# Two transformer blocks on one core: modulation scaled on ScalarE, attention divided at the end, gate work one expert pair earlier

## The chip, the core and the metric

The kernel runs on one NeuronCore of a Trainium2 chip. Five engines work side by side, each with its own queue that is served in order: TensorE (PE; its weight loads are PEld), VectorE (DVE), ScalarE (ACT), GpSimd (POOL), and SyncE (SP), which here only issues transfers. The metric is the device time of one execution in microseconds, the median of the runs. All matrices are fp32. Where a product of two matrices has to be exact, each factor is split into a rounded part and a rest (types `fp32r`), and three fast products take the place of one slow one.

## The reference

512 tokens of width 1024 go through two blocks. Cut to what matters here:

```python
mod = silu(c) @ ada_w + ada_b                  # six vectors of 1024: shifts, scales, gates
h = rmsnorm(x, g) * (1 + sc_a) + sh_a
# four mixers of four heads each: diff, forgetting ("fox"), stick-breaking, sparse ("nsa")
# forgetting attention, for a block of 128 queries:
s = q @ k.T * scale + (cum[query] - cum[key])  # cum: running sum of log forget gates
p = softmax(where(key <= query, s, NEG));  o = p @ v
x = x + gt_a * (concat(o_a, o_b, o_c, o_d) @ w_out)
x = x + gt_m * conv_ffn(rmsnorm(x) * (1 + sc_m) + sh_m)
# second block: pooling mixer and neighbourhood attention (softmax(s + bias) @ v), then
x = x + expert_choice_ffn(...)                 # 16 experts, 64 tokens each, silu(xe@wg) * (xe@wu) @ wd
g = sigmoid(rms_norm(x) @ w_ple_gate);  e = rms_norm(p @ w_ple_proj)
x = x + g * e                                  # gated embedding
```

## The kernel before

**Modulation.** The first 2048 columns of `ada_w` are done at the start. The other 4096 come as 64 tiles of 128 x 512 (`ada_more`, L349): SP loads tile `adw` (two buffers), POOL multiplies it by a column of `cT` (L355), and copies it into the accumulator `ada_a` (L358, first of each eight; one buffer) or adds it (L360). After eight tiles four small matmuls `pm` (L364) sum over the partitions. 48 tiles are spread over the mixers by `ada_side`, 16 belong to the loop of the conv FFN.

**Mixers of block one.** Eight cores (a mixer with two of its four heads) run two at a time as generators; between their steps, projections (`ftile`) of later mixers are recorded. A softmax goes: scores on PE; DVE adds the bias and finds the row minimum (`softmax_part`, L616); ACT takes the exponential and its row sum (L618); DVE forms 1/sum (L639) and scales the probabilities (`scale_parts`, L643); PE transposes them (`pt`), DVE or ACT copies them out of PSUM, PE multiplies by the values (`od`). In `fox` (L851) DVE also builds each bias in a tile `fb`: the key's running sum minus the query's (L861), and the causal mask on the last 128 keys (L862).

**Norms of heads.** `rstd_rows` (L379) makes one reciprocal root per token and group; with four groups it calls the six small instructions of `rstd_of` (L372 to L377) twice, for eight columns each. `to_features` (L388) lays such numbers along the free axis: a DVE copy to 128 x 512 (L393), four PE transposes into `rb` (L397).

**Block two.** Neighbourhood attention (`na`, L1184) has the same softmax chain, with 248 or 256 keys in a block.

**Experts.** Sixteen experts run as eight pairs, numbered 0 to 7; the two of a pair use the two column halves of PE side by side. A pair takes 48 weight chunks of 1 MB from HBM, loaded by SP into rings of buffers (`chy`, `chr`, `x16`, `chl`), 64 + 32 couples of matmuls (`ga`, `ua`, then `yd`), a scatter of its result to the tokens (`po`, `spread`), and the gather of the next pair's tokens `xg` (POOL, `route`). Beside that, in steps that `between` takes after each two chunks, goes the work of the gated embedding, in the list `todo`: `embedding()` in pair `E_AT`; `gate_base(t)` in the pairs of the table `BASE`, 16 couples of matmuls `pg` (L1553) of the tokens' state with the gate's weights `w_pg`; and `gate_pair`, from the first pair in `BASE` on, 16 couples `z` of the pair's own result with the same weights, scattered to those tokens whose base was taken before. `PACE` says how many steps `between` takes in each pair. From pair `RETIRE` on the six `chr` buffers hold `w_pg` and the gate's sums in place of chunks; POOL scales `w_pg` once (L1565). From pair `HOLD` = 4 on, these steps are tied behind the pair's own matmul in the recorded order; in earlier pairs the scheduling layer may move them.

**What sets the order.** Instructions are recorded in program order with priorities (`high_priority` shifts them), and a scheduling layer fixes each engine's queue from that before the run. Waits between engines are by semaphores; an engine stops at the first instruction whose input or buffer is not there.

Of the kernel before, what the change touches and what calls it, by code (L numbers as in the profile page):

```python
# [230 lines left out]
def _build(ctx, tc, nc, a, dbg, stop):  # L231
# [147 lines left out]
    def rstd_rows(sq, ind, n, scale, tag="dense"):  # L379
# [5 lines left out]
        for c in range(0, 4 * n, 8):  # L385
            rstd_of(ms[:, c:min(c + 8, 4 * n)], scale, y[:, c:min(c + 8, 4 * n)])
# [464 lines left out]
    def fox(hp):  # L851
        q, kk, v, ckb = st["fox", hp]
        o = ps("od", "o", 2)
        for i in range(4):
# [945 lines left out]
```

## Time and profile before

| | us |
|---|---|
| three runs | 2103.95, 2106.22, 2110.03; median 2106.22 |
| profiled execution, its own time | 2106.01 |
| its span, first to last instruction | 2104.2 |
| busy in the span: PE, DVE, ACT, POOL | 1904.4, 851.3, 555.5, 243.8 |
| start (norm, first projections) | 0 to 60 |
| mixers of block one and the second half of their output product | 60 to 470 |
| conv FFN | 470 to 850 |
| mixers of block two | 850 to 985 |
| output product, router | 985 to 1070 |
| expert pairs 0 to 7 | 1070 to 2074 |
| last gate and output | 2074 to 2104 |

Busy time is time in which an engine worked on an instruction; matmuls are pipelined, so a busy PE is not PE at its peak. The stages were told apart by the tiles in the timeline. In the rows below, `L643 DVE TENSOR_SCALAR e<-e,r` is an instruction of line 643 on DVE that writes tile `e` from `e` and `r`; `x64` says how many; behind the first bar stand their busy time and the mean of one in ns, behind the second the engine's idle time just before them and what ended most of it. The clock is the share of TensorE's full clock that was granted in the stretch.

### The profile page before, as it was taken

What the parts mean: (1) busy time and instruction counts of PE and PEld (TensorE: products, weight loads), DVE (VectorE), ACT (ScalarE), POOL (GpSimd) and SP (SyncE); (2) the same over time, 40 slices, a digit from 0 to 9 for tenths busy, and PEclk for the clock granted to TensorE, in tenths of its full rate; (3) what the DMA queues carried; (4) which work ended last, traced back from release to release, by engine and by line L of the source; (5) the groups of instructions that cost most, each with busy time, mean ns of one, the idle gap of its engine ahead of it and who ended that gap; (6) DMA issues with size and microseconds to landing.
All of it is one profiled execution on the core that took longest, in us unless ns stands there. A gap on an engine that the chain in (4) does not pass through costs nothing.

```text
span 2104.2 us, 22827 instructions
## 1 busy us (share of the span) xinstructions
PE 1904.4 (91%) x8822; PEld 1067.6 (51%) x8822; DVE 851.3 (40%) x1761; ACT 555.5 (26%) x1089; POOL 243.8 (12%) x211
## 2 busy tenths in 40 slices
PE   2898988979999999999989988988779999999997
PEld 1566656658888887777643322322223333333343
DVE  7887887875444335677441101210010020110114
ACT  4655544534323324445310000200000000100012
POOL 5540333350200000000100000000030000000001
PEclk9998998989999999999989999999989999999998
DMA  6532223333322223222589999899999999999991
GB/s 245 167 116 66 86 81 93 108 101 105 112 107 92 100 91 100 76 79 77 237 357 421 422 422 420 368 420 419 421 419 395 420 385 367 418 390 396 401 387 68
DMA packets 95084, 523.67 MB, mean 249 GB/s; under 512 B 11405, under 2 KB 12853, under 8 KB 44032
## 3 DMA queue, kind: packets, MB, share of 16 engines
q1 hardware_dynamic: 89936, 501.53, 60.9%
q0 software_dynamic: 3552, 17.82, 2.3%
q10 hardware_dynamic: 1488, 2.87, 0.4%
q8 instruction: 69, 1.13, 0.2%
q14 instruction: 39, 0.32, 0.0%
HBM read 510.83 MB, written 4.27 MB: 245 GB/s over the span
## 4 chain that ended last, share of the span: by engine, by line
PE 67%; DMA 18%; DVE 10%; ACT 2%; issue 2%; POOL 0%; SPq 0%; DVEq 0%; POOLq 0%; ACTq 0%
DMA ch<-in_w_ue_dram 8%; DMA ch<-in_w_de_dram 6%; PE ua L1697 5%; PE ga L1697 4%; PE ga L1698 4%; PE yd L1728 4%; PE yd L1727 3%; PE pg L1553 3%; PE z L1553 2%; PE ag L332 2%; PE ag L333 2%; PE ag L334 2%; PE od L649 2%; PE av L332 2%; PE av L333 2%; PE av L334 2%
## 5 line engine op out<-in xcount | busy, mean ns | idle before, releaser
L1697 PE MATMUL ga<-ch,xe 128*64 128x512 f32 x512 | 242.5, 610 | 9.0 <-DMA ch<-in_w_ge_dram 9.0
L1698 PE MATMUL ua<-ch,xe 128*64 128x512 f32 x512 | 231.1, 596 | 21.4 <-DMA ch<-in_w_ue_dram 21.4
L1728 PE MATMUL yd<-ch,hts 128*64 128x512 f32 (+1 forms) x544 | 233.5, 576 | 16.4 <-DMA ch<-in_w_de_dram 16.3
L1698 PE MATMUL ga<-ch,xe 128*64 128x512 f32 x512 | 236.5, 607 | 5.4 <-DMA ch<-in_w_ge_dram 5.4
L1727 PE MATMUL yd<-ch,hts 128*64 128x512 f32 (+1 forms) x544 | 234.8, 576 | 0.0
L1697 PE MATMUL ua<-ch,xe 128*64 128x512 f32 x512 | 233.5, 596 | 0.0
L325 DVE TENSOR_TENSOR wlo<-pan,whi 128x1024 fp32r<-128x1024 f32 x119 | 156.1, 1312 | 159.2 <-ACT whi L322 154.0
L322 ACT ACTIVATE whi<-pan 128x1024 fp32r<-128x1024 f32 x119 | 125.9, 1058 | 212.9 <-PE ag L333 93.8
L1708 DVE TENSOR_TENSOR sg<-sg,ua 128x512 f32<-128x512 f32 x32 | 22.0, 686 | 265.4 <-PE ua L1698 265.4
L1728 PEld LDWEIGHTS yd<-ch,hts 128*64 128x64 f32 x544 | 72.2, 138 | 110.4 <-issue 75.4
L1698 PEld LDWEIGHTS ga<-ch,xe 128*64 128x64 f32 x512 | 67.2, 139 | 93.3 <-issue 78.5
L1698 PEld LDWEIGHTS ua<-ch,xe 128*64 128x64 f32 x512 | 67.4, 137 | 88.7 <-issue 52.3
L1697 PEld LDWEIGHTS ua<-ch,xe 128*64 128x64 f32 x512 | 67.0, 137 | 77.0 <-issue 74.6
L338 DVE TENSOR_TENSOR ys<-yg,ys 128x512 fp32r<-128x512 f32 (+1 forms) x17 | 12.5, 733 | 229.9 <-ACT ys L337 229.9
L1697 PEld LDWEIGHTS ga<-ch,xe 128*64 128x64 f32 x512 | 66.0, 139 | 66.1 <-issue 54.0
L1727 PEld LDWEIGHTS yd<-ch,hts 128*64 128x64 f32 x544 | 71.6, 138 | 50.3 <-issue 47.9
L1687 ACT ACTIVATE hts<-pth 128x512 f32<-128x512 f32 x32 | 19.1, 596 | 266.9 <-PE pth L1686 266.9
L1731 ACT ACTIVATE yg<-yd,gs 128x512 f32<-128x512 f32 (+1 forms) x17 | 11.3, 662 | 287.2 <-PE yd L1728 196.3
L355 POOL TENSOR_TENSOR adw<-adw,cT 128x512 f32<-128x512 f32 x64 | 77.7, 1215 | 40.5 <-DMA adw<-in_ada_dram 40.3
L360 POOL TENSOR_TENSOR ada_a<-ada_a,adw 128x512 f32<-128x512 f32 x56 | 78.3, 1399 | 4.4
L1707 ACT ACTIVATE sg<-ga 128x512 f32<-128x512 f32 x32 | 19.1, 597 | 224.0 <-PE ga L1698 224.0
L618 ACT ACTIVATE e<-e,m 128x256 f32<-128x256 f32 (+8 forms) x128 | 65.1, 509 | 49.4 <-DVE m L616 46.9
(896 smaller groups left out, 3833.8 us busy)
## 6 DMA issues: line engine op xcount, KB each, us to landing
ch<-in_w_de_dram SPq DMA_DIRECT2D x128, 1024.0 KB, 13.7
ch<-in_w_ue_dram SPq DMA_DIRECT2D x125, 1024.0 KB, 9.9
ch<-in_w_ge_dram SPq DMA_DIRECT2D x120, 1024.0 KB, 13.4
pan<-in_w_up_dram SPq DMA_DIRECT2D x44, 512.0 KB, 3.2
adw<-in_ada_dram SPq DMA_DIRECT2D x64, 256.0 KB, 2.6
pan<-in_w_in_dram SPq DMA_DIRECT2D x24, 512.0 KB, 3.7
pan<-in_w_dn_dram SPq DMA_DIRECT2D x22, 512.0 KB, 3.2
adr<-in_adaT_dram SPq DMA_DIRECT2D x8, 1024.0 KB, 9.2
```

Source lines behind the costliest of these rows:

```text
L322: A.activation(hi, raw, AF.Copy)
L325: eng.tensor_tensor(lo, raw, hi.bitcast(FT), op=OP.subtract)
L332: T.matmul(out, wh, xh, start=first, stop=False)
L333: T.matmul(out, wh, xl, start=False, stop=False)
L334: T.matmul(out, wl, xh, start=False, stop=last)
L355: P.tensor_tensor(w, w, cT[:, k:k + 1].to_broadcast([128, 512]), op=OP.mult)
L360: P.tensor_tensor(ada_next[1], ada_next[1], w, op=OP.add)
L1553: T.matmul(out[c_], w[:, c_], x_, start=start, stop=stop)
L1697: T.matmul(acc_[m][0:64], xe[:, kk, 0:64], wa[:, k], start=kk == 0, stop=kk == 7)
L1698: mm = T.matmul(acc_[m][64:128], xe[:, kk, 64:128], wb[:, k], start=kk == 0, stop=kk == 7)
L1727: T.matmul(yd[0:64], hts[:, kk, 0:64], wa[:, k_], start=kk == 0, stop=kk == 15)
L1728: mm = T.matmul(yd[64:128], hts[:, kk, 64:128], wb[:, k_], start=kk == 0, stop=kk == 15)
```

## The change

Modulation: ACT multiplies the tile by the column (as the scale of a copy), writing the first of each eight straight into the accumulator; POOL keeps the additions. Forgetting attention: the query's term, the same for all keys of a row, is left out of the bias, since a softmax does not change with it; the mask is added once for both heads, into the key's tile, which makes the order of query blocks 3, 2, 1, 0. Forgetting and neighbourhood attention: the probabilities are not scaled; `divided` multiplies the output of all blocks by the reciprocals at the end, laid along the free axis by `to_features`. Norms: sixteen columns at a time. Experts: the tables move the gate's weights, bases and gating from pairs 4 to 7 to pairs 3 to 6 (gating still runs to pair 7), and the embedding from pair 2 to pair 1.

```diff
-RETIRE = 4
-BASE = {4: [0], 5: [1], 6: [2], 7: [3]}
-E_AT = 2
+RETIRE = 3
+BASE = {3: [0], 4: [1], 5: [2], 6: [3]}
+E_AT = 1
-PACE = [1.0, 1.0, 1.0, 1.0, 2.2, 2.2, 2.2, 2.2]
+PACE = [1.0, 1.0, 1.0, 2.2, 2.2, 2.2, 2.2, 1.5]
...
-            P.tensor_tensor(w, w, cT[:, k:k + 1].to_broadcast([128, 512]), op=OP.mult)
             if k == 0:
                 ada_next[1] = tmp[0].tile([128, 512], FT, name="ada_a", tag="ada_a", bufs=1)
-                P.tensor_copy(ada_next[1], w)
+                A.activation(ada_next[1], w, AF.Copy, scale=cT[:, 0:1])
             else:
+                A.activation(w, w, AF.Copy, scale=cT[:, k:k + 1])
                 P.tensor_tensor(ada_next[1], ada_next[1], w, op=OP.add)
...
-        for c in range(0, 4 * n, 8):
-            rstd_of(ms[:, c:min(c + 8, 4 * n)], scale, y[:, c:min(c + 8, 4 * n)])
+        rstd_of(ms[:, 0:4 * n], scale, y)
...
+    def divided(o, l, out):
+
+        A.activation(out, o, AF.Copy)
+        r = sm([128, 8], "r8", 2)
+        V.reciprocal(r, l)
+        V.tensor_tensor(out, out, to_features(r, 2), op=OP.mult)
...
     def fox(hp):
-        for i in range(4):
+        ls_ = sm([128, 4, 2], "l8", 2)
+        for i in (3, 2, 1, 0):
             nk = 128 * (i + 1)
+            V.tensor_tensor(ckb[:, :, nk - 128:nk], ckb[:, :, nk - 128:nk], K["cm"].unsqueeze(1).to_broadcast([128, 2, 128]),
+                            op=OP.add)
             for par in range(2):
-                h = 2 * hp + par
-                fb = t2k("fb")
-                V.tensor_scalar(fb[:, :nk], ckb[:, par, :nk], cqc[:, 4 * i + h:4 * i + h + 1], None, op0=OP.subtract)
-                V.tensor_tensor(fb[:, nk - 128:nk], fb[:, nk - 128:nk], K["cm"], op=OP.add)
                 s = ps("s", "s", 2)
                 scores(s, q, kk, par, slice(128 * i, 128 * i + 128), 0, nk)
-                e.append(softmax_part(s, fb[:, :nk], nk, l[:, par:par + 1]))
+                e.append(softmax_part(s, ckb[:, par, :nk], nk, ls_[:, i, par:par + 1]))
             yield
-            scale_parts(e, l, nk)
...
-        A.activation(mix[:, 2 + hp], o, AF.Copy)
+        divided(o, ls_.rearrange("p i h -> p (i h)"), mix[:, 2 + hp])
...
     def na(hp):
-            scale_parts(e, l, nk)
...
+        t = p2k("on")
+        divided(o, l.rearrange("p i h -> p (i h)"), t)
```

How the queues move, at the three places that the prediction speaks of. VectorE in forgetting attention of block one, before (`fb` is the bias, `e,m<-s,fb` the minimum, `r` and `e` of L641 and L643 belong to the sparse mixer beside it):

```order
L641 TENSOR_TENSOR r_3359<-r_3359,gates 128x2
L643 TENSOR_SCALAR e<-e,r_3359 128x31 x2
L634 COPY pts<-pt 31x128
L861 TENSOR_SCALAR fb<-ckb,cqc 128x128
L862 TENSOR_TENSOR fb<-fb,cst 128x128
L616 ISA e,m<-s,fb 128x128
L616 ISA m 128x1
```

and now (`ckb` is the key's tile with the mask):

```order
L615 ISA e,m<-s,ckb 128x256
L615 ISA m 128x1
L638 RECIPROCAL r_3019<-l_2921 128x2
L863 TENSOR_TENSOR ckb<-ckb,cst 128x2x128
L640 TENSOR_TENSOR r_3019<-r_3019,gates 128x2
L642 TENSOR_SCALAR e<-e,r_3019 128x384 x2
```

The two bias instructions ahead of each minimum became one mask addition per block; the scaling that is left is that of the sparse mixer. ScalarE at the end of the mixers, where the output product's panels are split (`whi`) and the squares for the next norm are taken (`sq`), before:

```order
L923 ACTIVATE mix<-od 128x512
L337 ACTIVATE hTh<-mix 128x512
L322 ACTIVATE whi<-pan 128x1024
L408 ACTIVATE sq<-x 128x512 x3
L322 ACTIVATE whi<-pan 128x1024
L408 ACTIVATE sq<-x 128x512 x2
```

and now:

```order
L337 ACTIVATE hTh<-mix 128x512
L322 ACTIVATE whi<-pan 128x1024
L357 ACTIVATE ada_a<-adw,cT 128x512
L359 ACTIVATE adw<-adw,cT 128x512 x2
L407 ACTIVATE sq<-x 128x512
L322 ACTIVATE whi<-pan 128x1024
L359 ACTIVATE adw<-adw,cT 128x512
L407 ACTIVATE sq<-x 128x512
```

Eight modulation tiles, recorded for the loop of the conv FFN, stand between the squares and panels. TensorE where pair 3 begins, before (`po` scatters the pair before):

```order
L1728 MATMUL yd<-ch,hts 64x512
L1697 MATMUL ga<-ch,xe 64x512
L1537 MATMUL po<-ys,ott 128x512 x4
L1698 MATMUL ga<-ch,xe 64x512
L1697 MATMUL ga<-ch,xe 64x512
```

and now (`ptg` turns the tokens of a base, `pg` is the base's product):

```order
L1731 MATMUL yd<-ch,hts 64x512
L1540 MATMUL po<-ys,ott 128x512 x8
L1606 MATMUL ptg<-cst,xk 128x128 x8
L1556 MATMUL pg<-ch 64x512 x17
L1700 MATMUL ga<-ch,xe 64x512
L1556 MATMUL pg<-ch 64x512 x6
L1701 MATMUL ga<-ch,xe 64x512
```

More than half of the first base's 32 matmuls stand ahead of the pair's first own matmul. On GpSimd the eight scalings of `w_pg`, one run of eight before, now stand in runs of two, two and four, with the gather of pair 4's tokens and the copies that wait for it in between.

## Rows read from the trace of the kernel before

**Rows 1.** Stretches: us, busy us of PE, PEld, DVE, ACT, POOL; clock, DMA share, GB/s.
```profile
60.00:470.00 410.00, 356.63 (x1884) 256.81 (x1884) 328.44 (x814) 205.89 (x496) 147.75 (x118) 0.94 0.31 99
850.00:985.00 135.00, 133.54 (x692) 102.89 (x692) 97.89 (x253) 63.15 (x144) 1.61 (x3) 1.00 0.25 80
```

**Rows 2.** Chain of waits, 60 to 470: share of the stretch by engine and line.
```profile
by line: PE od L649 6.1%; PE pt L627 5.6%; issue 3.7%; DVE e L643 3.6%; PE ms L383 3.2%; DVE wlo L325 3.1%; PE s L817 2.4%; DVE e L616 2.4%; PE od L920 2.3%; DVE e L706 1.8%; DVE q L576 1.6%; PE rb L397 1.4%; DVE fb L862 1.3%; DVE sq L410 1
```

**Rows 3.** Groups by line, VectorE, 60 to 470: busy us, mean ns, idle before.
```profile
L325 DVE TENSOR_TENSOR wlo<-pan,whi 128x1024 fp32r<-128x1024 f32 x31 | 44.8, 1444 | 5.7 <-issue 2.7 <-ACT whi L322 2.6 <-PE acc__1241 L334 0.3
L643 DVE TENSOR_SCALAR e<-e,r 128x128 f32<-128x128 f32 (+7 forms) x64 | 32.9, 550 | 0.6
L410 DVE TENSOR_TENSOR sq<-sq 128x512 f32<-128x512 f32 x7 | 10.4, 1479 | 2.2 <-ACT sq L408 2.2
L861 DVE TENSOR_SCALAR fb<-ckb,cqc 128x128 f32<-128x128 f32 (+3 forms) x16 | 9.0, 560 | 0.0
L862 DVE TENSOR_TENSOR fb<-fb,cst 128x128 f32<-128x128 f32 x16 | 8.4, 526 | 0.3
L376 DVE TENSOR_TENSOR rv<-rv,ry 128x8 f32<-128x8 f32 (+2 forms) x19 | 3.7, 201 | 0.3
L568 DVE SCALAR_TENSOR_TENSOR sq<-pr,cols,rb 128x512 f32<-128x512 f32 x5 | 3.7, 741 | 0.9 <-PE rb L397 0.9
```

**Rows 4.** The same view, VectorE, 850 to 985.
```profile
L325 DVE TENSOR_TENSOR wlo<-pan,whi 128x1024 fp32r<-128x1024 f32 x16 | 19.5, 1220 | 0.4 <-ACT whi L322 0.2
L643 DVE TENSOR_SCALAR e<-e,r 128x248 f32<-128x248 f32 (+1 forms) x22 | 6.8, 345 | 0.1
L393 DVE COPY bc<-rs 128x512 f32<-128x512 f32 x8 | 3.4, 426 | 0.2
L568 DVE SCALAR_TENSOR_TENSOR sq<-pr,cols,rb 128x512 f32<-128x512 f32 x4 | 3.0, 740 | 0.6 <-PE rb L397 0.6
```

**Rows 5.** The same view, VectorE, 818 to 850.
```profile
L410 DVE TENSOR_TENSOR sq<-sq 128x512 f32<-128x512 f32 x7 | 4.9, 694 | 0.0
```

**Rows 6.** The same view, GpSimd, 60 to 470.
```profile
L355 POOL TENSOR_TENSOR adw<-adw,cT 128x512 f32<-128x512 f32 x58 | 69.4, 1198 | 38.3 <-DMA adw<-in_ada_dram 38.2
L360 POOL TENSOR_TENSOR ada_a<-ada_a,adw 128x512 f32<-128x512 f32 x49 | 69.3, 1414 | 3.8
L358 POOL COPY ada_a<-adw 128x512 f32<-128x512 f32 x7 | 6.7, 958 | 182.9 <-PE pm L364 182.9
```

**Rows 7.** The same view, ScalarE, 60 to 470.
```profile
L408 ACT ACTIVATE sq<-x 128x512 f32<-128x512 f32 x8 | 4.9, 627 | 11.6 <-DVE x L1014 11.6
L495 ACT ACTIVATE xn<-xin,shf,amul 128x512 f32<-128x512 f32 x2 | 1.6, 818 | 0.7 <-DVE amul L493 0.7
```

**Rows 8.** The same view, TensorE, 850 to 985.
```profile
L397 PE MATMUL rb<-cst,bc 128*128 128x128 f32 x32 | 5.8, 274 | 0.0
```

**Rows 9.** Stretches as in rows 1: expert pairs 3 to 7.
```profile
1418.00:1547.50 129.50, 96.29 (x425) 32.11 (x422) 12.08 (x16) 9.77 (x15) 10.16 (x8) 0.97 1.01 420
1547.50:1676.70 129.20, 122.61 (x533) 41.06 (x533) 12.21 (x21) 9.53 (x15) 6.85 (x6) 0.97 1.00 410
1676.70:1810.70 134.00, 130.75 (x574) 45.90 (x573) 16.63 (x27) 10.59 (x17) 1.31 (x3) 0.97 0.96 386
1810.70:1940.60 129.90, 128.99 (x580) 44.66 (x579) 18.53 (x31) 10.76 (x18) 1.32 (x3) 1.00 0.99 397
1940.60:2074.20 133.60, 133.59 (x654) 55.67 (x655) 22.08 (x37) 15.30 (x33) 0.00 (x0) 1.00 0.85 339
```

**Rows 10.** Chain of waits in order of time: start us, us, what; pair 5.
```profile
1738.07 1.02 PE ptg L1603 x8
...
1768.37 2.57 PE pg L1553 x12
```

**Rows 11.** Timeline of GpSimd, 1536 to 1580: start us, us, what, idle before.
```profile
1537.69 15.29 POOL L1565 TENSOR_TENSOR ch<-ch,cols 128x1024 f32<-128x1024 f32 x8 [118.11 <-DMA ch<-in_w_pg_dram]
...
1572.86 0.42 POOL L1483 COPY gs<-xg 64x1 f32<-64x1 f32 x2 [7.69 <-DMA xg<-xd,at]
```

More of the change, by code (lines that the diff above doesn't have):

```diff
@@ L369, in rstd_of @@
     def rstd_of(acc, scale, out, n=128):
-        v, y = sm([128, 8], "rv")[0:n, 0:out.shape[-1]], sm([128, 8], "ry")[0:n, 0:out.shape[-1]]
+        v, y = [sm([128, 16], n_, 4)[0:n, 0:out.shape[-1]] for n_ in ("rv", "ry")]
         V.tensor_scalar(v, acc, scale, EPS, op0=OP.mult, op1=OP.add)
@@ L723, in _build @@
     cum = pa.tile([4, S], FT, name="cum")
-    cqc = pa.tile([128, 16], FT, name="cqc")
     def gates_and_decay():
@@ L740, in gates_and_decay @@
         V.tensor_tensor_scan(cum, f2[0:4], f[0:4], 0.0, op0=OP.mult, op1=OP.add)
-        V.tensor_copy(t[0:4], cum)
         pg = ps("pg", "pt", 2)
@@ L747, in gates_and_decay @@
         V.tensor_scalar(gates[:, 0, 0:4], gates[:, 0, 0:4], K["vcol"], None, op0=OP.mult)
-        V.tensor_copy(cqc.rearrange("p (t c) -> p t c", t=4), pg[:, :, 0:4])
     def compress(kv):
@@ L853, in fox @@
         o = ps("od", "o", 2)
-        for i in range(4):
+        ls_ = sm([128, 4, 2], "l8", 2)
+        for i in (3, 2, 1, 0):
             nk = 128 * (i + 1)
-            l = sm([128, 2], "l2")
             e = []
+            V.tensor_tensor(ckb[:, :, nk - 128:nk], ckb[:, :, nk - 128:nk], K["cm"].unsqueeze(1).to_broadcast([128, 2, 128]),
+                            op=OP.add)
             for par in range(2):
-                h = 2 * hp + par
-                fb = t2k("fb")
-                V.tensor_scalar(fb[:, :nk], ckb[:, par, :nk], cqc[:, 4 * i + h:4 * i + h + 1], None, op0=OP.subtract)
-                V.tensor_tensor(fb[:, nk - 128:nk], fb[:, nk - 128:nk], K["cm"], op=OP.add)
                 s = ps("s", "s", 2)
                 scores(s, q, kk, par, slice(128 * i, 128 * i + 128), 0, nk)
-                e.append(softmax_part(s, fb[:, :nk], nk, l[:, par:par + 1]))
+                e.append(softmax_part(s, ckb[:, par, :nk], nk, ls_[:, i, par:par + 1]))
             yield
-            scale_parts(e, l, nk)
             pts = [transpose_p(e[par], nk, par) for par in range(2)]
@@ L1186, in na @@
         o = ps("od", "o", 2)
+        l = sm([128, 4, 2], "l8", 2)
         for b in range(4):
             nk = 248 if b else 256
-            l = sm([128, 2], "l2")
             e = []
@@ L1198, in na @@
                     T.matmul(s[:, :nk], q[:, par, 128 * b:128 * b + 128], k_, start=x_ == 0, stop=x_ == 1)
-                e.append(softmax_part(s, nb[:, par, 0:248] if b else nb[:, par, 248:], nk, l[:, par:par + 1]))
+                e.append(softmax_part(s, nb[:, par, 0:248] if b else nb[:, par, 248:], nk, l[:, b, par:par + 1]))
             yield
-            scale_parts(e, l, nk)
             pts = [transpose_p(e[par], nk, par) for par in range(2)]
@@ L1205, in na @@
             yield
-        m, o = mix2[:, 4 + hp].rearrange("p (r c) -> p c r", r=8), o.rearrange("p (c r) -> p c r", r=8)
+        t = p2k("on")
+        divided(o, l.rearrange("p i h -> p (i h)"), t)
+        m, o = mix2[:, 4 + hp].rearrange("p (r c) -> p c r", r=8), t.rearrange("p (c r) -> p c r", r=8)
         A.activation(m[:, 0:56], o[:, 8:], AF.Copy)
```

## The prediction

> **What bounds the kernel now.** I cut the span into stages and read the busy times of each stage, since the share over the whole span mixes stages with different limits. From 60 to 470, the mixers of block one, TensorE works 356.6 of 410 us and VectorE 328.4; neither is full, and the clock is 0.94 of full speed; from 850 to 985, the mixers of block two, TensorE works 133.5 of 135 [rows 1]. So in the second stretch only TensorE's work counts, and in the first the two engines wait for each other in turn. The chain of waits there shows it: links of PE (`od`, `pt`) alternate with links of VectorE (`e` of L643 3.6%, `wlo` 3.1%, `e` of L616 2.4%, `fb` 1.3%) [rows 2]. The groups by line then give the price of one instruction: for VectorE in the mixers of block one [rows 3], in those of block two [rows 4] and in a piece of the FFN [rows 5], for GpSimd [rows 6] and ScalarE [rows 7].
>
> In the expert pairs the reader is to compare PE's busy time with the length of the pair: pair 3 is held by transfers (96.3 us of work in 129.5 at 420 GB/s), pair 4 nearly (122.6 in 129.2), pairs 5 to 7 by TensorE (130.8 of 134.0, 129.0 of 129.9, 133.6 of 133.6) [rows 9].
>
> **Mixers of block one: VectorE's own work.** Removed: 16 subtractions of L861, 9.0 us, and 16 mask additions of L862, 8.4; the two forgetting cores' share of the scalings, 16 of the 64 of L643 at 0.550, 8.8 [rows 3]. In the norms with four groups one set of small instructions goes: I count four such sites, four VectorE instructions each at 0.2 (L376 [rows 3]), 3.2. Added: eight mask additions over both heads, 128 x 2 x 128; two widths of 128 in one instruction were not run, so I take 0.55 (between L862's 0.526 for one width and 1.05 for two), 4.4. Added at the end of each of the two cores: a reciprocal (0.2), the copy `bc` (0.43) and a product that reads PSUM, for which L568 of the same size stands at 0.74 [rows 4]; 2.7 for both. Together -9.0 - 8.4 - 8.8 - 3.2 + 4.4 + 2.7 = -22.3 us.
>
> **The same stretch: what GpSimd takes from VectorE.** The same addition of L410 takes 1.479 us from 60 to 470 [rows 3] and 0.694 from 818 to 850 [rows 5]; `wlo` takes 1.444 against 1.220 in block two [rows 4]. In the slow stretch GpSimd is at work 147.8 us, in block two 1.6 [rows 1]. By these differences VectorE loses 7 x 0.785 = 5.5 on L410, 31 x 0.224 = 6.9 on L325, and at most 64 x 0.205 = 13.1 on L643 (its shapes differ, so this is an upper end), and on the bias lines some 3 that I put in proportion; about 29 in all. Of GpSimd's 145.4 us in its three lines the change takes L355 and L358, 69.4 + 6.7 = 76.1, or 52% [rows 6]. The value I take is 52% of 29 plus a little for lines not counted, -16; the bounds are 0 (the slowdown stays, because the additions that remain read two tiles each) and -29.
> The Trainium skill ("GPSIMD Engine Reference", Specifications) says that GpSimd shares its SBUF interfaces with VectorE, with contention for VectorE instructions in a two-port mode or with two SBUF inputs. The two times of L410 agree, and so does L568, whose product reads one input from PSUM: 0.741 in this stretch [rows 3] and 0.740 in block two [rows 4]. By the rule the additions that stay on GpSimd go on slowing VectorE while they run, so that the sum holds the -16 and not the -29.
>
> **How much of it reaches the end.** -22.3 - 16 = -38 us of VectorE's work. For three lines both views have a number: the chain holds 3.6, 3.1 and 1.3% of 410, that is 14.8, 12.7 and 5.3 us, out of 32.9, 44.8 and 8.4 busy [rows 2, 3]: 32.8 of 86.1, or 38%. 0.38 x 38 = -14.5. The rest is hidden by TensorE's own work, which holds the chain the other times; that cover is not lost, since PE's work hardly changes: four transposes `rb` for each core, 8 at 5.8/32 = 0.18 [rows 8], +1.5. The clock: with shorter pauses I expect 0.95 in place of 0.94 (1.00 where PE is full [rows 1]), 356.6 x 0.01 = -4.
>
> ScalarE takes over 58 scalings of 128 x 512, with a pointer as scale. Without a pointer such an instruction takes 0.627, with two 0.818 [rows 7]; I take 0.72, so 42 us on an engine that is busy 205.9 of 410 [rows 1]. They fall between exponentials that PE waits for. Below: 0, if each finds a gap. Above: the 38% of VectorE, 16 us. What queues behind a scaling that waits for its tile is the next exponential, and behind that `pt` and `od` on PE. GpSimd waited 38.2 us for `adw` [rows 6] and held up nobody; on ScalarE the same wait would. But the layer puts the instruction where it expects the tile, and the tile's buffer is free sooner, as two engines now share the work: +2. L357 also inherits the wait of L358 for `pm` (182.9 [rows 6]): that is mostly the pause between groups of eight, so I price it at nothing; if not, it is part of the second rival.
> The Trainium skill ("ScalarE: Activation LUTs", Rules for kernel authors) advises a multiplication on VectorE and not on ScalarE. By that advice the 42 us would be some 28 us of VectorE's (an estimate by the copy of 0.426 in rows 4, with a little added), on the fuller of the two engines, so the trace speaks for ScalarE here.
>
> Mixers of block one: -14.5 + 1.5 - 4 + 2 = -15. Bounds: -53, all of TensorE's idle time, and +30 (second rival).
>
> **Mixers of block two.** The scalings leave VectorE, 22 in the row's 6.8 us [rows 4], but PE works 133.5 of 135 and hides them. PE gets 16 transposes `rb` at 0.18 = +2.9, of which some may fall into the 1.5 idle us; I take +2; range -5 (the chain through VectorE does count) to +6 (two ends of core where PE waits for copy, `rb` and product, 0.43 + 0.27 + 0.74 each, and the copy out of `on`).
>
> **Experts.** A base is 16 couples `pg` of four records each: 12 records in 2.57 us make 0.857 for a couple, so 13.7 us, and eight `ptg` take 1.0 [rows 10]. The loads of `w_pg`, 4 MB, now stand ahead of pair 3's chunks and not pair 4's: at 420 GB/s [rows 9] that is 10.0 us. So pair 3 starts its own chunks at 1418.0 + 10.0 = 1428.0. Pairs 3 to 6 carry what 4 to 7 carried: I take 129.2, 134.0, 129.9 and, for pair 6, their mean 131.0. Pair 7 keeps `z` and loses the base: 133.6 - 13.7 - 1.0 = 118.9; the bytes of rows 9 (339 x 133.6 = 45.3 MB) would need 381 GB/s, below the 420 seen. End of pairs: 1428.0 + 129.2 + 134.0 + 129.9 + 131.0 + 118.9 = 2071.0, against 2074.2: -3. There is one gating step more (its couples `z`, and `po` pairs for the scatter), and it is hidden where PE had waited for transfers, 33 us in pair 3. What hides less is the start: scaling `w_pg` takes GpSimd 15.3 us, and now stands around the copies `gs`, which waited 7.7 for the gather [rows 11]. 15.3 + 7.7 = 23 us against 10 in which the weights land: the last weight is some 12 us late, with 17 `pg` ahead of the pair's first `ga`. I cost it at nothing beyond old pair 4, which had the same run of scalings in its 129.2. Bounds: -20 (PE's sum of rows 9 is 612.2 in 656.2 us, so the pairs could close up by nearly half of that gap) and +8 (the third rival). The embedding moves from a pair held by transfers to another: 0.
>
> **Sum.** The profiled run took 2106.0, the median of the runs is 2106.2, so no correction. -15 + 2 - 3 = -16: 2090.
>
> **Rivals.**
> - VectorE decides in the mixers throughout. For: DVE 328.4 of 410 and a clock below 1. Against: PE lines head the chain. All 38 us come: -38 + 1.5 - 4 + 2 + 2 - 3 = -39.5: 2066.
> - ScalarE's queue takes the place (the slower side). Place: the exponentials between 60 and 470 and the squares and panel splits at 440 to 470, where the order puts modulation between them. Price: half of GpSimd's wait of 38.2, 19, and 38% of 42, 16: 35 in place of the 2: -15 + 33 = +18; with +2 - 3: 2123. It decides once ScalarE costs more than 18 us, the 2 and the 16 that the sum gains. Against: ScalarE is half idle.
> - Pair 3's start isn't caught up: the 12 us stay, as PE is 98 to 99% busy in the pairs after (130.8 of 134.0, 129.0 of 129.9) and has no room: 2090 + 12 = 2102. For: pair 4's slack was 6.6 us. Against: that slack already held the same run of scalings.
> - The relief isn't to be had: the two-tile additions of GpSimd that remain slow VectorE as much, and TensorE covers its shorter work. Left are the bias lines' link, 5.3 - 4.4, so -1, +1.5 for `rb`, +2, -3: 2105.5.
>
> **Chances.** Forecast 0.44, with a range of its own of 2080 to 2099; VectorE throughout 0.18; relief not to be had 0.18; ScalarE 0.12; pair 3 0.08. A measurement can tell about 0.3%, 6.3 us, from no change: faster is below 2099.9, slower above 2112.5. Faster: 0.42 + 0.18 + 0.05 + 0.04 = 0.69; same: 0.02 + 0.11 + 0.02 + 0.04 = 0.19; slower: 0.02 + 0.10 = 0.12. Range: 2063 to 2112, which leaves out the far half of the ScalarE case and the deep end of VectorE's.
>
> **What would show it.** In the profile after: L410's mean (now L409) near 1.1 in the mixers, `wlo` near 1.33 and VectorE about 290 busy in the same stretch; the clock there at 0.95. ScalarE near 248, with little idle time put down to `adw`; much of it would be the second rival. `rb` 16 more in block two, that stage 2 us longer. Pair 3's first `ga` some 10 us later than the last `yd` before it, pair 7 near 119 us. The forecast is wrong if the stage of the mixers ends later than before, or if the pairs take longer than 1000 us.

## The result, and the profile after

The changed kernel takes 2084.0 us (median of four, 2082.4 to 2087.7) against 2107.7 before: a ratio of 0.989, interval 0.987 to 0.991. Forecast were 2090 and a range of 2063 to 2112. The profiled execution spans 2081.8 us, 22.4 less than before. By stages (the first `ag` of the FFN, the last `dn`, the first `ga` and the last `yd` are the cuts):

| us | before | after | forecast |
|---|---|---|---|
| 60 to the FFN's first `ag` | 408.2 | 381.0 | -15 |
| FFN | 366.3 | 366.5 | 0 |
| mixers of block two, router | 235.9 | 236.2 | +2 |
| expert pairs | 1003.9 | 1008.7 | -3 |

So the sum came out near by luck, from two terms that were both off: the mixers of block one gained 27, not 15, and the pairs lost 5 where 3 were to be gained.

Stretches of the kernel after, columns as in [rows 1]; the first is block one's mixers to the FFN's first instructions, the second block two's:

```profile
60.00:443.00 383.00, 356.78 (x1893) 261.34 (x1892) 284.14 (x754) 239.24 (x544) 71.33 (x53) 0.93 0.34 105
823.00:958.00 135.00, 133.58 (x700) 103.39 (x700) 94.66 (x225) 62.69 (x142) 1.62 (x3) 0.99 0.26 80
```

TensorE's busy time in the first stretch is what it was (356.8 after 356.6); 27 us of its idle time are gone. VectorE fell from 328.4 to 284.1, GpSimd from 147.8 to 71.3, ScalarE rose by 33. The clock did not rise. The second stretch was cut to the same 135 us as before; TensorE's busy time in it is unchanged, and the whole stage in the table is 0.3 longer with the 16 added transposes in it. Groups by line, VectorE, 60 to 443, against [rows 3] (each line number is one lower):

```profile
L325 DVE TENSOR_TENSOR wlo<-pan,whi 128x1024 fp32r<-128x1024 f32 x31 | 39.5, 1276 | 6.2 <-ACT whi L322 5.6 <-PE acc__936 L334 0.3
L642 DVE TENSOR_SCALAR e<-e,r 128x128 f32<-128x128 f32 (+7 forms) x48 | 17.4, 397 | 0.6
L409 DVE TENSOR_TENSOR sq<-sq 128x512 f32<-128x512 f32 x7 | 7.5, 1070 | 2.1 <-ACT sq L407 2.1
L863 DVE TENSOR_TENSOR ckb<-ckb,cst 128x256 f32<-128x256 f32 x8 | 3.4, 422 | 0.1
L376 DVE TENSOR_TENSOR rv<-rv,ry 128x8 f32<-128x8 f32 (+3 forms) x15 | 2.5, 164 | 0.2
```

The mean of the adder of squares is the 1.1 us that the prediction named, `wlo` with 1.276 is better than its 1.33, and the scalings lost 15.5 us, which is what the prediction's two terms give them together (8.8, and half of at most 13.1). ScalarE's groups there show the price of the new scaling and its wait:

```profile
L359 ACT ACTIVATE adw<-adw,cT 128x512 f32<-128x512 f32 x50 | 35.2, 716 | 12.4 <-DMA adw<-in_ada_dram 12.2
L357 ACT ACTIVATE ada_a<-adw,cT 128x512 f32<-128x512 f32 x7 | 5.0, 719 | 4.0 <-PE pm L364 3.9
```

0.716 us each, as taken (0.72), and 12.2 us of idle time for tiles. The chain of waits, 60 to 443, shows what of it is on the path:

```profile
by line: PE od L655 8.2%; PE pt L626 5.7%; PE s L820 3.1%; PE ms L383 2.8%; ACT whi L322 2.3%; issue 2.0%; DVE wlo L325 1.9%; PE rb L396 1.9%; DMA adw<-in_ada_dram 1.5%; PE ck L849 1.5%; PE s L597 1.3%; DVE e L642 1.2%; PE s L704 1.1%; PE o
```

VectorE's `e` went from 3.6 to 1.2% and `wlo` from 3.1 to 1.9% [rows 2]; `fb` is gone. New is the transfer of `adw` with 1.5% of 383, 5.7 us. Its size is not to be trusted: in four kernels below that share these mixers, the chain holds 3.1 to 16.6 us of it.

### The profile page after: what moved, and what is told of

Same layout as the page of the kernel before. It is cut to its first block, busy times and chain, and to the rows that moved or that the text cites. A ratio compares the mean times of both kernels' runs of the same rounds, so it can differ in the third digit from the quotient of the medians.

```text
span 2081.8 us, 23062 instructions
## 1 busy us (share of the span) xinstructions
PE 1926.1 (93%) x8934; PEld 1082.0 (52%) x8934; DVE 808.8 (39%) x1677; ACT 596.7 (29%) x1151; POOL 158.4 (8%) x139
## 4 chain that ended last, share of the span: by engine, by line
PE 70%; DMA 13%; DVE 5%; issue 2%; ACT 2%; POOL 1%; POOLq 0%; DVEq 0%; SPq 0%; ACTq 0%
DMA ch<-in_w_ue_dram 7%; PE ua L1700 6%; PE ga L1701 5%; PE ga L1700 5%; PE yd L1730 4%; DMA ch<-in_w_de_dram 4%; PE yd L1731 3%; PE z L1556 3%; PE pg L1556 3%; PE od L655 2%; PE ag L332 2%; PE ag L333 2%; PE ag L334 2%; PE av L332 2%; PE po L1540 2%
## 5 line engine op out<-in xcount | busy, mean ns | idle before, releaser
L1701 PE MATMUL ua<-ch,xe 128*64 128x512 f32 x512 | 231.3, 596 | 18.5 <-DMA ch<-in_w_ue_dram 18.4
L1700 PE MATMUL ga<-ch,xe 128*64 128x512 f32 x512 | 237.7, 600 | 0.0
L1730 PE MATMUL yd<-ch,hts 128*64 128x512 f32 (+1 forms) x544 | 236.2, 578 | 0.0
L1701 PE MATMUL ga<-ch,xe 128*64 128x512 f32 x512 | 232.6, 599 | 3.1 <-DMA ch<-in_w_ge_dram 3.1
L325 DVE TENSOR_TENSOR wlo<-pan,whi 128x1024 fp32r<-128x1024 f32 x119 | 149.6, 1258 | 163.0 <-ACT whi L322 160.5
L360 POOL TENSOR_TENSOR ada_a<-ada_a,adw 128x512 f32<-128x512 f32 x56 | 77.3, 1380 | 380.3 <-ACT ada_a L357 273.2
L1556 PE MATMUL z<-ch,yt 128*64 128x512 f32 x320 | 92.2, 603 | 1.3 <-DVE yt L1741 1.3
```

Source lines behind the costliest of these rows:

```text
L325: eng.tensor_tensor(lo, raw, hi.bitcast(FT), op=OP.subtract)
L1556: T.matmul(out[c_], w[:, c_], x_, start=start, stop=stop)
L1700: T.matmul(acc_[m][0:64], xe[:, kk, 0:64], wa[:, k], start=kk == 0, stop=kk == 7)
L1701: mm = T.matmul(acc_[m][64:128], xe[:, kk, 64:128], wb[:, k], start=kk == 0, stop=kk == 7)
L1730: T.matmul(yd[0:64], hts[:, kk, 0:64], wa[:, k_], start=kk == 0, stop=kk == 15)
```

## The experiments

Twelve kernels, which ran in three groups, each beside the kernel before (median 2105.0, 2107.7 and 2106.9 us there); the ratio is to the kernel before in the same group, and kernels of different groups are best compared by it. "Mixers" is the profiled run's time from 60 to the first `ag`, "PE idle" the part of it in which TensorE had no matmul (matmuls that the trace lacks make it longer), "pairs" the time of the expert pairs; "slowed" is worked out from the records of the mixers: for each VectorE instruction that overlaps one of GpSimd, its time less the fifth percentile of its form, summed. The mixers of one and the same program took 381.0, 384.5, 379.9 and 382.2 in the four kernels from "changed" to `hold3` that share it, so one reading is good to some 2.5 us; their idle time of TensorE is 25.4 to 28.2. The rest of the stage is TensorE's busy time, which for the same products changes with the clock. Every kernel that changes the mixers also has their queues in another order, so a difference of a few us in the stage need not be the edit's alone.

| kernel | median us | ratio, interval | mixers | PE idle | VectorE busy | slowed | GpSimd busy | clock | pairs |
|---|---|---|---|---|---|---|---|---|---|
| before | 2107.7 | | 408.2 | 53.3 | 326.7 | 63.4 | 147.7 | 0.94 | 1003.9 |
| changed | 2084.0 | 0.987-0.991 | 381.0 | 26.2 | 282.2 | 25.5 | 71.3 | 0.93 | 1008.7 |
| no_tables | 2075.0 | 0.983-0.988 | 384.5 | 28.2 | 281.9 | 25.2 | 71.2 | 0.93 | 997.9 |
| embed_early | 2075.8 | 0.982-0.989 | 379.9 | 25.4 | 280.8 | 24.1 | 71.3 | 0.94 | 1001.0 |
| hold3 | 2077.4 | 0.982-0.988 | 382.2 | 26.6 | 282.5 | 26.1 | 71.2 | 0.93 | 1003.7 |
| tables_only | 2113.1 | 1.001-1.005 | 409.7 | 51.0 | 326.6 | 63.4 | 149.0 | 0.92 | 1009.8 |
| act_only | 2077.7 | 0.984-0.989 | 384.0 | 34.8 | 286.7 | 21.6 | 71.4 | 0.94 | 1000.2 |
| att_only | 2096.0 | 0.993-0.997 | 400.0 | 44.4 | 312.3 | 57.9 | 150.2 | 0.93 | 1002.1 |
| rstd_only | 2121.2 | 1.005-1.010 | 416.6 | 52.1 | 323.7 | 59.0 | 153.4 | 0.92 | 1001.1 |
| pool_again | 2085.7 | 0.986-0.993 | 392.7 | 36.9 | 302.1 | 45.9 | 138.2 | 0.94 | 1001.0 |
| dve_one | 2074.4 | 0.981-0.987 | 380.3 | 28.9 | 288.5 | 0.1 | 3.4 | 0.94 | 1000.8 |
| dve_no_att | 2086.3 | 0.988-0.994 | 385.9 | 36.1 | 299.4 | 0.1 | 3.4 | 0.93 | 998.8 |
| late | 2074.4 | 0.982-0.989 | 376.5 | 27.1 | 280.5 | 23.0 | 61.2 | 0.95 | 999.9 |
| dve_late | 2073.3 | 0.982-0.987 | 376.9 | 27.7 | 284.3 | 0.1 | 3.4 | 0.95 | 1001.5 |

### One part at a time

**tables_only**: before, with the tables of the pairs.

```diff
-RETIRE = 4
-BASE = {4: [0], 5: [1], 6: [2], 7: [3]}
-E_AT = 2
+RETIRE = 3
+BASE = {3: [0], 4: [1], 5: [2], 6: [3]}
+E_AT = 1
```

(and `PACE` as in the change.) 

> The kernel before with the new tables of the expert pairs alone. Theory: the profile of the changed kernel has its expert pairs 4.9 us longer (1008.7 against 1003.9 us), and nothing outside the pairs causes that, so the tables alone cost +5 us: about 2112 us, with pair 1 some 14 us longer and pair 7 some 11 us shorter. Rival (the sum of the prediction): -3 us, the longer pairs of the changed kernel being due to the earlier part of the program.

Measured: as the theory, 2113.1, 0.3% slower (interval 0.1 to 0.5%), pairs 1009.8, pair 1 12.8 longer and pair 7 10.8 shorter. The tables cost by themselves.

**no_tables**: the changed kernel with these lines as before.

```diff
-RETIRE = 3
+RETIRE = 4
```

(and the other three.) 

> The changed kernel with the tables of the expert pairs as before. Theory: the whole gain of 27 us lies before the conv FFN, so the time is about 2080 us, less than the changed kernel's, and the FFN starts near 440 us from the start of the span. Rival (the sum of the prediction): the tables gain 3 us, so the time is about 2087 us.

Measured: 2075.0, below the theory's 2080: the pairs took 997.9, 11 less than in the changed kernel. The tables' price is 5 to 11 us: ten kernels with the old tables take 997.9 to 1003.9 for the pairs, 1000.7 on average, and the two with the new ones and `HOLD` as before 1008.7 and 1009.8.

**act_only**: before, with the modulation's hunk.

```diff
-            P.tensor_tensor(w, w, cT[:, k:k + 1].to_broadcast([128, 512]), op=OP.mult)
-                P.tensor_copy(ada_next[1], w)
+                A.activation(ada_next[1], w, AF.Copy, scale=cT[:, 0:1])
+                A.activation(w, w, AF.Copy, scale=cT[:, k:k + 1])
```

> The kernel before with the modulation's multiplication on ScalarE alone. Theory: GpSimd's work slows VectorE's two-input instructions, so the mean of L325 falls from 1.444 to about 1.28 us and that of L410 from 1.479 to about 1.1, VectorE is some 15 us less busy, and the stage of the mixers gets shorter by 6 to 12 us. Rival: the waits of ScalarE's queue for the tiles take it back; the stage is as long as before or longer, by up to 10 us.

Measured: far more than the theory's 6 to 12. This one part gives 24 us in the mixers (408.2 to 384.0), 18.5 of them TensorE's idle time, with VectorE 40 us less busy, though not one of VectorE's 811 instructions was removed. The rival with the waits for tiles is out here, and so is the prediction's "relief isn't to be had". Three of its lines, 60 to 444, against [rows 3]:

```profile
L643 DVE TENSOR_SCALAR e<-e,r 128x128 f32<-128x128 f32 (+7 forms) x64 | 24.0, 415 | 0.8
L861 DVE TENSOR_SCALAR fb<-ckb,cqc 128x128 f32<-128x128 f32 (+3 forms) x16 | 7.7, 478 | 0.0
L862 DVE TENSOR_TENSOR fb<-fb,cst 128x128 f32<-128x128 f32 x16 | 4.6, 289 | 0.3
```

The same 64 scalings cost 24.0 in place of 32.9, the same mask additions 4.6 in place of 8.4.

**att_only**: before, with `fox`, `na` and `divided` alone.

```diff
-                V.tensor_scalar(fb[:, :nk], ckb[:, par, :nk], cqc[:, 4 * i + h:4 * i + h + 1], None, op0=OP.subtract)
-                V.tensor_tensor(fb[:, nk - 128:nk], fb[:, nk - 128:nk], K["cm"], op=OP.add)
+            V.tensor_tensor(ckb[:, :, nk - 128:nk], ckb[:, :, nk - 128:nk], K["cm"].unsqueeze(1).to_broadcast([128, 2, 128]), op=OP.add)
-            scale_parts(e, l, nk)
+        divided(o, ls_.rearrange("p i h -> p (i h)"), mix[:, 2 + hp])
```

> The kernel before with forgetting and neighbourhood attention changed alone (no query term, one mask addition, division at the end). Theory: VectorE loses the instructions that the prediction counted, about 19 us of busy time or more with GpSimd still beside it, and six tenths of that reach the end, as in the whole change (27 of 46): 11 to 16 us shorter mixers of block one, block two unchanged. Rival: the whole 27 us of the mixers come from this part, and the modulation's move gives nothing.

Measured: 8.2 us in the mixers with VectorE 14.4 less busy: less than the theory's range, and far from the rival's 27. Alone the two parts take 40.0 and 14.4 us from VectorE, together 44.5: partly the same time, since an instruction that is gone can't be slowed any more. Whether the stage shows that too is open: its two gains sum to 32 against 27, within the spread of the readings, and TensorE's idle time falls by 18.5 and 8.9, 27.4 together, and by 27.1 in the changed kernel.

**rstd_only**: before, with sixteen columns of a norm at once (the small tiles `rv` and `ry` get 16 columns and four buffers in place of 8 and eight).

```diff
-        for c in range(0, 4 * n, 8):
-            rstd_of(ms[:, c:min(c + 8, 4 * n)], scale, y[:, c:min(c + 8, 4 * n)])
+        rstd_of(ms[:, 0:4 * n], scale, y)
```

> The kernel before with the norms of sixteen columns in one go alone. Theory: 16 small VectorE instructions of 0.2 us and 8 of ScalarE go, 3 us of VectorE, six tenths to the end: 2 us, which the times cannot tell from none; VectorE's count of L372 falls from 19 to 15 in the mixers. Rival: each of these links is on a serial chain with ScalarE's two between, so four whole sets of about 1.3 us reach the end: 5 us.

Measured: neither. VectorE has the 3.0 us less and 16 instructions fewer, yet the kernel is 0.7% slower (interval 0.5 to 1.0%). The stretch 60 to 476.6:

```profile
60.00:476.60 416.60, 364.48 (x1882) 266.07 (x1881) 323.68 (x795) 203.81 (x488) 153.44 (x118) 0.92 0.31 97
```

TensorE is busy 9.6 us more for the same products, at a clock of 0.92 for 0.94: 354.9 x 0.94/0.92 = 362.6, so most of it is the clock; its idle time is 1.2 shorter. The queues of the mixers stand in another order than before; whether that, or the fewer buffers, makes TensorE pause where the clock then falls is open. So an edit that takes work away made a stage 8 us longer, as much as `att_only` gained and `pool_again` below lost; there, unlike here, TensorE's idle time moved too, by 9 us each.

### GpSimd against VectorE

In the trace of before, the timeline of VectorE and of GpSimd at 326 us (start, length, instruction):

```profile
326.08 2.60 DVE L643 TENSOR_SCALAR e<-e,r 128x384 f32<-128x384 f32 x2
328.60 0.54 DVE L616 CUSTOM_DVE_ANT_0 e<-s,fb 128x384 f32<-128x384 f32 x1
```

```profile
326.09 1.26 POOL L360 TENSOR_TENSOR ada_a<-ada_a,adw 128x512 f32<-128x512 f32 x1
327.31 1.15 POOL L355 TENSOR_TENSOR adw<-adw,cT 128x512 f32<-128x512 f32 x1
328.54 1.27 POOL L360 TENSOR_TENSOR ada_a<-ada_a,adw 128x512 f32<-128x512 f32 x1
```

Two scalings that take 0.41 us each when alone take 2.60: each ends some 0.2 us after the GpSimd instruction beside it. The delay is thus not a share of VectorE's instruction but the rest of GpSimd's; even a scaling of 128 x 23 took 0.98 in place of 0.22. The next instruction, which reads its scores from PSUM, runs beside the third GpSimd instruction and takes 0.54, the mean of its form being 0.55. Nor is every instruction within SBUF held up. Two of the same 128 x 2 tile, over the whole kernel (shortest, median, longest in ns):

```profile
L639 DVE RECIPROCAL r<-l x48: 139/158/167, 188.9 to 1004.3; 128x2 f32<-128x2 f32 x48
L641 DVE TENSOR_TENSOR r<-r,gates x24: 150/160/954, 190.3 to 364.7; 128x2 f32<-128x2 f32 x24
```

The reciprocal with its one input is never slow, though eight of them began during a GpSimd instruction; the product with two is.

**pool_again**: GpSimd gets its load back, ScalarE keeps the scaling (no_tables plus one instruction).

```diff
+            P.tensor_tensor(ada_next[1], ada_next[1], K["ones"].to_broadcast([128, 512]), op=OP.mult)
```

> The changed kernel with the old tables of the pairs, and one more GpSimd instruction behind each addition of the modulation: a multiplication of the accumulator by ones, of the form and size of the old L355; ScalarE keeps the scaling. Theory: VectorE instructions that move data from SBUF to SBUF wait until a GpSimd instruction that has begun is over; with some 60 us of GpSimd work back, VectorE is 20 to 28 us busier in the mixers, and six tenths of that reach the end: the stage is 12 to 17 us longer, about 2089 us against 2075. Rival: the gain of the modulation's move came from tiles that turn round faster, as two engines share them, and GpSimd's load is nothing to VectorE: within 3 us of 2075.

Measured: GpSimd +67.0, VectorE +20.2 us busy, slowed 45.9 after 25.2, the mixers 8.2 longer, the time 2085.7, between the theory's 2089 and the rival. The mechanism is shown for VectorE's busy time: load on GpSimd alone does it. What reaches the end is 0.41 of VectorE's time against `no_tables`, and 0.53 against the mean of the four kernels with its mixers (381.9): less than the six tenths I had expected, within what one reading can be off. ScalarE also waits 3.4 us longer for tiles here (17.2 after 13.8), a part that these runs don't separate. Groups by line, VectorE, 60 to 453:

```profile
L325 DVE TENSOR_TENSOR wlo<-pan,whi 128x1024 fp32r<-128x1024 f32 x31 | 42.4, 1368 | 6.8 <-ACT whi L322 6.1 <-PE acc__940 L334 0.3
L643 DVE TENSOR_SCALAR e<-e,r 128x128 f32<-128x128 f32 (+7 forms) x48 | 21.1, 477 | 0.6
L410 DVE TENSOR_TENSOR sq<-sq 128x512 f32<-128x512 f32 x7 | 9.7, 1390 | 2.2 <-ACT sq L408 2.2
```

**dve_one**: no_tables with the rest of the modulation on VectorE.

```diff
-                A.activation(w, w, AF.Copy, scale=cT[:, k:k + 1])
-                P.tensor_tensor(ada_next[1], ada_next[1], w, op=OP.add)
+                V.scalar_tensor_tensor(ada_next[1], w, cT[:, k:k + 1], ada_next[1], op0=OP.mult, op1=OP.add)
```

> The changed kernel with the old tables, in which VectorE takes the modulation's multiplication and addition in one instruction (the first of each eight stays on ScalarE), so that GpSimd has nothing of it. Theory (VectorE and GpSimd exclude each other, six tenths of VectorE's time reach the end): VectorE loses the 25 us that the additions still cost it in the mixers and gets 49 instructions of about 0.74 us, 36 us; net +11, so +7 us for the end, less the 6 us of waits for tiles that ScalarE has on the chain: 2074 to 2082. Rival: what GpSimd costs VectorE is gone already, so the whole 36 us come, and 22 of them reach the end: 2095 or more.

Measured: as the theory, 2074.4; VectorE has 49 instructions of 0.75 us more in the mixers and is only 6.6 us busier, since nothing slows it now:

```profile
60.00:440.30 380.30, 351.40 (x1890) 261.35 (x1889) 288.50 (x800) 208.57 (x493) 3.36 (x4) 0.94 0.35 106
```

The Trainium skill's advice to multiply on VectorE and not on ScalarE ("ScalarE: Activation LUTs", Rules for kernel authors) gives the same time here, because it also empties GpSimd. (36.6 us of work less 25.1 of slowdown would be 11.5; the other 5 us are not accounted for.)

**dve_no_att**: before with that modulation, attention and norms old (the same diff against the kernel before). 

> The kernel before with the modulation on VectorE in one instruction, attention and norms as before. Theory (instructions priced without GpSimd beside them: 16 of 0.34, 16 of 0.28, 16 of 0.42 and 16 of 0.2 removed by the rest of the change, 6.1 us added, so 13.5 us of VectorE, six tenths to the end): 8 us more than the 2074.4 with them: about 2082. Rival: the rest of the change is worth what it is beside ScalarE's scaling, 2.7 us between two runs: about 2077.

Measured: 2086.3, 12 us above `dve_one`, more than the theory's 8; in the profiled runs the mixers differ by 5.6 and VectorE by 10.9. The rest of the times' difference goes with the clock, which was 0.967 to 0.972 over the span in its four runs and 0.974 to 0.978 in those of `dve_one`. So with GpSimd silent the rest of the change, attention and norms, is worth 6 to 12 us; the work that it takes from VectorE itself fits that (TensorE's idle time differs by 7.2), but how much of the time is the clock's is not shown.

### ScalarE's wait at the end of the mixers

**late** and **dve_late**: no_tables and `dve_one`, in which the last 16 tiles use a copy of the column that exists only once the FFN's input does.

```diff
+            cT = tcs["cT"] if m < 48 else tcs["cT2"]
+    V.scalar_tensor_tensor(tcs["cT2"], hTh[:, 7, 0:8].bitcast(FT), 0.0, tcs["cT"], op0=OP.mult, op1=OP.add)
     for j in range(22):
```

> The changed kernel with the old tables, in which the last 16 modulation tiles, recorded for the loop of the conv FFN, get a second copy of the column that depends on the last features of the FFN's input, so that they can't stand between the squares and panels at the end of the mixers. Theory (the second rival of the prediction, in small): there ScalarE waits for tiles on the path, about 6 us in the chain of the changed kernel, so the time falls from 2075 to about 2069. Rival: those waits lie beside TensorE's own work of the output product: within 2 us of 2075.

> As the one before, with VectorE taking multiplication and addition in one instruction. Theory: VectorE has 7 instructions of 0.75 us less at the end of the mixers, 5 us, of which half to six tenths reach the end, and the FFN hides them, since TensorE holds it: 2070 to 2072 against the 2074 without the delay. Rival: VectorE's panel splits in the FFN are late and TensorE waits: 2076 or more.

Measured: the mixers take 376.5 and 376.9, the shortest of all; the FFN stays at 365.6 and 366.8. The times are 2074.4 (runs from 2069.4 to 2080.9) and 2073.3. For `late` this is the rival's "within 2 us of 2075", and `dve_late` falls between its theory and its rival. The shorter stretch does not show that a wait is gone either. Stretches of `no_tables` and of `late`, columns as in [rows 1]:

```profile
60.00:444.50 384.50, 356.26 (x1890) 261.02 (x1889) 281.93 (x751) 237.51 (x543) 71.22 (x53) 0.93 0.34 105
60.00:436.50 376.50, 349.36 (x1893) 256.91 (x1891) 280.54 (x751) 231.25 (x535) 61.24 (x46) 0.95 0.34 102
```

TensorE's idle time is 27.1 us in `late` and 25.4 to 28.2 in the four kernels without the delay; 6.9 of the 8 us between these two rows are its busy time at another clock, and the profile of `late` is that of its fastest run. `dve_late` has the lowest median here; its interval lies below that of the changed kernel, but not below those of `dve_one` and `no_tables`, which have the same old tables.

### The pairs

Pairs 1 and 2 before, then pairs 1, 2, 3 and 7 after, columns as in [rows 9]:

```profile
1173.30:1285.90 112.60, 97.53 (x430) 33.58 (x426) 12.29 (x21) 8.62 (x14) 1.91 (x4) 0.98 1.01 421
1285.90:1418.00 132.10, 113.56 (x489) 38.29 (x490) 23.40 (x38) 16.65 (x33) 1.31 (x3) 0.99 0.97 399
```

```profile
1146.70:1273.70 127.00, 113.97 (x493) 38.16 (x490) 23.43 (x38) 16.82 (x33) 1.33 (x3) 0.96 0.95 393
1273.70:1415.50 141.80, 114.17 (x479) 38.79 (x477) 17.66 (x27) 11.99 (x18) 16.92 (x13) 0.96 1.01 420
1415.50:1541.30 125.80, 107.33 (x482) 37.37 (x479) 6.12 (x9) 7.41 (x12) 0.00 (x0) 0.97 0.94 383
...
1929.70:2052.50 122.80, 121.65 (x583) 49.35 (x583) 22.28 (x37) 14.29 (x32) 0.00 (x0) 1.00 0.89 369
```

With the embedding pair 1 is 14 longer; pair 2, freed of it, should be some 12 shorter plus 10 for `w_pg`, and is 10 longer. Its end on TensorE after (timeline):

```profile
1391.62 1.02 PE L1731 MATMUL yd<-ch,hts 128*64 128x512 f32 x2
...
1400.96 3.84 PE L1556 MATMUL pg<-ch 128*64 128x512 f32 x16
1406.97 1.08 PE L1556 MATMUL pg<-ch 128*64 128x512 f32 x4 [2.17 <-POOL ch L1568]
1408.82 6.89 PE L1556 MATMUL pg<-ch 128*64 128x512 f32 x16 [0.77 <-POOL ch L1568]
1415.52 0.59 PE L1700 MATMUL ga<-ch,xe 128*64 128x512 f32 x1
```

and on GpSimd:

```profile
1396.89 3.75 POOL L1568 TENSOR_TENSOR ch<-ch,cols 128x1024 f32<-128x1024 f32 x2
1404.53 0.42 POOL L1486 COPY gs<-xg 64x1 f32<-64x1 f32 x2 [3.89 <-DMA xg<-xd,at]
1405.02 7.44 POOL L1568 TENSOR_TENSOR ch<-ch,cols 128x1024 f32<-128x1024 f32 x4
```

23 us lie between the last `yd` and the first `ga`; TensorE stands before the base and waits for scalings behind the gather. With the old tables the pause for `w_pg` stands before pair 4 and is 8.8 us long:

```profile
1547.46 1.97 PE L1697 MATMUL ga<-ch,xe 128*64 128x512 f32 x2 [8.83 <-DMA ch<-in_w_ge_dram]
```

In the 23 us the transfers go on at full rate, into the rings (419 GB/s from 1392 to 1400); then they all but stop, where in `hold3` below they do not. The stretch 1416 to 1424 after, and in `hold3`:

```profile
1416.00:1424.00 8.00, 8.00 (x40) 3.07 (x37) 0.00 (x0) 0.00 (x0) 0.00 (x0) 1.00 0.20 61
1416.00:1424.00 8.00, 8.00 (x33) 2.94 (x34) 2.57 (x7) 0.00 (x0) 0.99 (x1) 1.00 1.01 419
```

So pair 3 moves 383 GB/s where 420 bound it before.

**embed_early**: no_tables, but `E_AT = 1`.

```diff
-E_AT = 2
+E_AT = 1
```

> The changed kernel with the old tables of the pairs, but for the embedding, which goes in the second pair. Theory: pair 1 gets some 13 us longer and pair 2 some 12 shorter, both held by transfers: 2075, within 3 us. Rival: the embedding's move is what lengthens the pairs of the changed kernel, so the pairs take 5 to 11 us more: 2080 to 2086.

Measured: 2075.8, as the theory; pair 1 125.2, pair 2 121.0. The embedding's place is free of charge.

**hold3**: the changed kernel with the steps of pair 3 tied behind its own matmuls.

```diff
-HOLD = 4
+HOLD = 3
```

> The changed kernel with HOLD = 3, so that the steps of pair 3 too are tied behind the pair's own matmuls. Theory: in the changed kernel TensorE begins the base of pair 3 before the pair's own work and waits there for GpSimd's scaling of the weights, 23 us from the last yd to the first ga, in which the rings fill and transfers stop; tied behind the pair's matmuls this is covered, and the pairs take 8 to 14 us less: 2070 to 2076. Rival: the pairs are longer because of the work that was added, wherever it stands: 2081 to 2087.

Measured: 2077.4, pairs 1003.7: 5 to 6 us of the tables' price come back, less than expected. Whether the old tables stay ahead is not shown: 1003.7 lies within the 997.9 to 1003.9 of the ten kernels that have them. TensorE at the start of pair 3:

```profile
1401.69 1.97 PE L1700 MATMUL ga<-ch,xe 128*64 128x512 f32 x2 [8.82 <-DMA ch<-in_w_ge_dram]
```

The first `ga` now comes 8.8 us after the last `yd`, near the 10 that the prediction had assumed for the change itself.

## Why the prediction was right and where it was not

- **VectorE's busy time: -38 forecast, -44.5 measured** (326.7 to 282.2), but made up otherwise. The step "what GpSimd takes from VectorE" took the difference on four lines, about 29 us, and half of it. The pairs of rows were right: with GpSimd silent (`dve_no_att`) L643, L325 and L410 take 0.345, 1.219 and 0.688. But the slowdown of all lines was 63 us, and the change took 38 of these. "VectorE's own work" was priced from rows in which these instructions had themselves been slowed; with GpSimd silent the bias lines take 0.379 for 0.560 and 0.287 for 0.526 and the scalings 0.345 for 0.550, so of the 26.2 us removed about 16 were work and 10 were relief, a part of which the -16 counts again. The bound of -29 was too near: it left out every line of which I had no two rows.
- **How much reaches the end: 0.38 forecast, 27.2/44.5 = 0.61 measured.** This is the term that was off most: the 0.38 came from three lines' share of one chain. `act_only` gives 24.2/40.0 = 0.61, `att_only` 8.2/14.4 = 0.57, `pool_again` 0.41 to 0.53. Why it is more than the chain says is not shown; that shortening a link of VectorE also ends the wait of the next one is a guess. The chain is a poor measure of it: VectorE's links in the chain of the mixers sum to 125 us before, and to 45, 73, 57 and 49 in the four kernels that share the changed mixers. The gain of 27 lies midway between my 15 and the 38 of the case "VectorE decides throughout", to which I gave 0.18; "the relief isn't to be had", also 0.18, is refuted by `act_only`.
- **The clock: -4 forecast, nothing measured.** 0.93 after 0.94 in the stretch.
- **ScalarE: +2 forecast.** The scalings cost 0.716 as taken; 5.7 us of waits for tiles are in the chain, at the place that the second rival names. That they cost the kernel anything is not shown: `late` brings ScalarE's idle time for tiles from 13.8 us (`no_tables`) to 6.0, and TensorE's idle time stays. The price is far below the rival's point of decision (18).
- **Mixers of block two: +2 forecast, 0.3 measured**: the 16 transposes came (`rb` 48 in the stage for 32, 8.4 us for 5.8), and which work gave way is not shown.
- **Experts: -3 forecast, +5 measured, by 6 to 11 in other pairs of runs.** The step that failed is "I cost it at nothing beyond old pair 4": its run of scalings lay behind pair 4's own matmuls, which `HOLD` ties; in pair 3 nothing ties them, and the order shown ahead of the prediction had 17 `pg` before the first `ga`. This is the third rival (12 us, 0.08), and `hold3` shows its cause. What remains in `hold3`, 3 us above the forecast's 1001, stands in pair 7: 123.4 us, with TensorE busy for 122.3, where the prediction had 118.9. There the term "loses the base" was mis-sized; the gating step that was added would do it (TensorE is busy 945.7 us in the pairs after, and 925.6 before), but no run takes it away alone.
- **The signs.** Near what was named: L409, `wlo`, VectorE's 284 for "about 290", ScalarE's 239 for 248, `rb` in block two, the end of the mixers. Missed: the clock, the first `ga` of pair 3 (23 us for 10), pair 7 (122.8 for 119). By its last sign, pairs above 1000 us, the forecast of the pairs is wrong; that sign was set too tight, as the sum itself has 2071.0 - 1070 = 1001.

The total was right within 6 us by luck: the mixers' surplus (12) and the pairs' shortfall (8) have opposite signs.

## What to carry to other kernels

Count a helper engine's cost by what it does to the others: here 76 us of an engine that was idle most of the time held 40 us of VectorE's and some 24 of the stage's. Price what you remove as it will stand without the load that you also remove, or you count the relief twice. Where an order is given, read what stands before the first instruction that a transfer feeds, and ask which rule of the planner had kept it behind.

## What the runs showed of the hardware

- VectorE and GpSimd shut each other out for many instructions from SBUF to SBUF: a scaling of 128 x 23 that began during a GpSimd multiplication took 0.98 us in place of 0.22, and one of 128 x 384 during an addition 1.42 in place of 0.41. It goes the other way too: the 14 GpSimd additions before that began with no such VectorE instruction at work took 1.26 to 1.30 us, the others up to 2.15, behind a panel split. Additions of two inputs are hit, and so is the scaling with one; the reciprocal with one (0.139 to 0.167) and instructions that read PSUM (L568 0.741 and 0.740) are not. The Trainium skill ("GPSIMD Engine Reference", Specifications) names two SBUF inputs or a two-port mode as the conditions; the trace agrees for two inputs, no run here shows in which mode the scaling worked, and the loss is the rest of the other engine's instruction.
- The granted clock differs between executions of one program, and in some programs the time goes with it: `rstd_only` ran from 2112.3 us at 0.969 to 2124.4 at 0.961, `late` from 2069.4 at 0.978 to 2080.9 at 0.969. It is not the whole: the fastest of `att_only`'s five runs, 2092.4, has its lowest clock, 0.970. After the 8.8 us pause in `hold3` the granted clock is 0.50, the lower of its two levels, from 1401.6 to 1408.0, with `ga` of 1.06 to 1.11 us; from 1408 to 1415 it is 0.98, with `ga` of 0.59:

```profile
1401.60:1408.00 6.40, 5.79 (x12) 1.53 (x14) 0.00 (x0) 0.00 (x0) 5.61 (x4) 0.50 1.01 421
1408.00:1415.00 7.00, 7.00 (x27) 2.02 (x23) 1.23 (x2) 0.60 (x1) 0.00 (x0) 0.98 1.01 420
```
